# Two-block transformer kernel, one core: gate units, buffers and engines at the start of the seven-product stage

## The chip, the cores and the metric

The kernel runs on 1 core of one Trainium2 chip. The metric is the device time of one execution in microseconds (us). Engine names are those of the profile: PE is TensorE's matmul, PEld its weight load, DVE is VectorE, ACT is ScalarE, POOL is GpSimd, SP is SyncE, which issues nearly all DMAs.

## What is computed

The reference runs two blocks of two layers each on a sequence of 1024 tokens of width 1024, in float32. The change touches only block 1, whose layer is, cut to what matters:

```python
proj = h @ w_in
(aq, ak, av, az, cx, cb, cc, cz, rq, rk, rv, rz, gates) = split(proj)
a = diff_attention(aq, ak, av, ...) * silu(az)
c = short_conv(cx, cb, cc, conv_w) * silu(cz)
r = retention(rq, rk, rv) * silu(rz)
g = sigmoid(gates).reshape(b, s, 3, 1024)
merged = g[:, :, 0] * (a @ w_branch[0])
for i in range(1, 3):
    merged = merged + g[:, :, i] * ((a, c, r)[i] @ w_branch[i])
return x + merged @ w_out
```

The columns `gates` are 3072 wide: 24 units of 128 columns.

## The kernel before

**Arithmetic.** All matmuls are split: an operand x becomes a high part (`c.hi`, a ScalarE copy to the fast matmul type, L144) and a low part x - high (`c.lo`, a subtraction, L151, on VectorE or GpSimd), and a product is three matmuls, high-high, high-low and low-high (`mm3`, L177 to L179). The tokens stand in the free dimension, in two halves f = 0, 1 of 512. The normed input is H[f][k], k = 0 to 7, as tile pairs `hh{f}_{k}`, `hl{f}_{k}`.

**Stages of a block 1 layer.** Attention with the short convolution's units in its gaps (pool C, and A and AZ in it), retention (pool R, also inside C), the gates (pool GS inside pool G), the branch merge (GM inside G), the output product (W). Pools are stacked: pool G opens where pool C began, so its first tiles lie on C's tiles (`cth` 2 KB per partition, then `u`, then `y`, some 4 KB each, all of the convolution), the next ones on R's. With `reuse_waits="tile"` a tile waits only for the older tiles that lie where it lies. Tags of a pool are laid in the order in which they are first asked for. A tag with n buffers hands them out in turn, and a new tile waits for the last reader of the one that held its buffer.

**A plain unit** (`c.unit`, L181) multiplies 128 weight columns with one half: 8 x 3 = 24 matmuls into one of two PSUM banks `pj0`, `pj1` in turn, 48 matmuls for both halves. Weights are loaded to `wr` (2 buffers) and split into `wh` and `wl` (3 buffers each, L166).

**A pair by seven products** (`c.seven`, L230) computes two units with both halves as a 2x2 block product with seven block multiplications in place of eight: 7 x 4 x 3 = 84 matmuls. Its right-hand operands are blocks of H (`B["11"]`, `["21"]`, `["22"]`) and four combinations t1 to t4, computed once per layer; its left-hand ones are made for each pair by `pair_weights` (L198). It opens with product 1 into a `pb` bank, copied to `m` by L242, then product 2 with t2; t3 comes in product 4, t1 in product 5, t4 in product 6. The `pb` tag has four banks.

**The gates stage before** (L810 to L850). Two plain units (44, 45), then 11 pairs. The operands: for each k of 0 to 3, four sums high + low (b12, b22 on VectorE, b11, b21 on GpSimd, L832), four differences (L834, L836, L837, L839) and three splits (t3's low part on GpSimd, those of t2 and t4 on VectorE). They use the tags `m`, `u3`, `c21` and `sc`, two buffers each, and write the tiles t2, t3, t4 (`slot`, pool G). t1 is split later, onto H[1][0 to 3], after the plain units have read those. `gate` (L811) applies tanh on ScalarE to a bank (L813) and stores the result to DRAM (L815); for plain units and for the first gate of a pair it writes to a tile of tag `sc`.

**The merge** (GM, L870 on): for 24 pairs (branch, d) it loads two gates to `gt` (L875), multiplies branch tiles (loaded through `br`, L863) with weights into a `pb` bank, and sums on VectorE (L886 for the first branch). In the kernel before, `gt` is the first tag of GM and lies on the first tags of GS, `m` and `u3`.

**Order.** TensorE runs in program order in these stages (`manual()`); the other engines and SyncE run in the order that a scheduler chose when the program was built, each strictly in that order.

Of the kernel before, what the change touches and what calls it, by code (L numbers as in the profile page):

```python
# [10 lines left out]
F32 = mybir.dt.float32  # L11
# [3 lines left out]
ALU = mybir.AluOpType  # L15
# [4 lines left out]
P = 128  # L20
T = 1024
HW = 512
# [390 lines left out]
def block1_layer(c, a, l, H, rest, last):  # L413
    nc = c.nc
    v, g, s = nc.vector, nc.gpsimd, nc.scalar
# [5 lines left out]
    def load_unit(u):  # L421
        return c.weights(a["w1"][l, u], 1024)

    def manual():
        return c.tc.manual_schedule(engines={mybir.EngineType.PE})
# [103 lines left out]
    with c.scope("C") as pc:  # L529

        with c.scope("A") as pa:
# [14 lines left out]
            gs = c.t(pa, "gs", [P, 1])  # L546
# [259 lines left out]
    with c.scope("G") as pg:  # L806
        def slot(nm, k):
            return tuple(c.t(pg, f"{nm}{x}_{k}", [P, HW], F32R) for x in "hl")

        with c.scope("GS") as pq, manual():  # L810
            def gate(u, f, src, dst=None):  # L811
                dst = c.t(pq, "sc", [P, HW], bufs=2) if dst is None else dst
                s.activation(dst, src, AF.Tanh, scale=0.5)  # L813
                gsp[u, f] = c.dram([P, HW], "sg")
                nc.sync.dma_start(out=gsp[u, f], in_=dst)  # L815

            def split(x, hl, eng):
                c.hi(hl[0], x)
                c.lo(hl[1], x, hl[0], eng=eng)
                return hl  # L820

            def pair(j):
                return c.pair_weights(a["w1"][l, 44 + 2 * j], a["w1"][l, 45 + 2 * j], 1024, pq)

            ws0 = [load_unit(44 + u) for u in range(2)]
            B = {"11": H[0][:4], "21": H[0][4:], "22": H[1][4:], "t1": [], "t2": [], "t3": [], "t4": []}
            t1 = []
            for k in range(4):
                b12, b11, b22, b21 = (c.t(pq, x, [P, HW], F32, 2) for x in ("m", "u3", "c21", "sc"))
                for x, (f, kk), eng in ((b12, (1, k), v), (b22, (1, k + 4), v), (b11, (0, k), g), (b21, (0, k + 4), g)):  # L830
                    hh, hl = H[f][kk]
                    eng.tensor_tensor(out=x, in0=hh.bitcast(F32), in1=hl.bitcast(F32), op=ALU.add)  # L832
                t1.append(c.t(pq, "t1", [P, HW], F32, 4))
                v.tensor_tensor(out=b22, in0=b22, in1=b12, op=ALU.subtract)  # L834
                B["t3"].append(split(b22, slot("t3", k), g))
                v.tensor_tensor(out=t1[k], in0=b12, in1=b11, op=ALU.subtract)  # L836
                v.tensor_tensor(out=b11, in0=b22, in1=b11, op=ALU.add)  # L837
                B["t2"].append(split(b11, slot("t2", k), v))
                v.tensor_tensor(out=b21, in0=b21, in1=b11, op=ALU.subtract)  # L839
                B["t4"].append(split(b21, slot("t4", k), v))  # L840
            for u in range(2):
                for f in range(2):
                    gate(u, f, c.unit(ws0[u], H, f))
                if u == 0:
                    nxt = pair(1)
            for k in range(4):
                B["t1"].append(split(t1[k], c.htile(1, k), v))
            for j in range(1, 12):
                ws, nxt = nxt, pair(j + 1) if j < 11 else None
                c.seven(ws, B, pq, lambda i, f, x: gate(2 * j + i, f, x, None if (i, f) == (0, 0) else x))  # L850


        def branch(br):

            places = ((lambda k: c.htile(0, k), lambda k: slot("t2", k)),
                      (lambda k: c.htile(0, 4 + k), lambda k: slot("t3", k)),
                      (lambda k: slot("t4", k), lambda k: slot("t2", k)))[br]
            out = []
            for f in range(2):
                out.append([])  # L860
                for i in range(4):
                    raw = c.t(pg, "br", [P, HW], bufs=2)
                    nc.sync.dma_start(out=raw, in_=spill[br, i][f])  # L863
                    hl = places[f](i)
                    c.hi(hl[0], raw)
                    c.lo(hl[1], raw, hl[0])
                    out[f].append(hl)
            return out

        with c.scope("GM") as pq, manual():  # L870
            merged, nxt, B = {}, c.weights(a["wb"][l, 0, 0], 512), branch(0)
            for br, d in [(br, d) for br in range(3) for d in range(KD)]:
                gt = [c.t(pq, "gt", [P, HW], bufs=4) for _ in range(2)]
                for f in range(2):
                    nc.sync.dma_start(out=gt[f], in_=gsp[8 * br + d, f])  # L875
                (wh, wl), n = nxt, KD * br + d + 1
                if n < 3 * KD:
                    nxt = c.weights(a["wb"][l, n // KD, n % KD], 512)
                if d == 3 and br < 2:
                    Bn = branch(br + 1)  # L880
                for f in range(2):
                    ps = c.psb()
                    c.product(ps, (wh, wl), 0, B[f])
                    if br == 0:
                        merged[f, d] = c.t(pq, f"mg{f}_{d}", [P, HW])
                        v.scalar_tensor_tensor(out=merged[f, d], in0=gt[f], scalar=1.0, in1=ps, op0=ALU.add, op1=ALU.mult)  # L886
                    else:
                        mt = merged[f, d]
                        v.scalar_tensor_tensor(out=gt[f], in0=gt[f], scalar=1.0, in1=ps, op0=ALU.add, op1=ALU.mult)
                        v.tensor_tensor(out=mt, in0=mt, in1=gt[f], op=ALU.add)  # L890
                if d == KD - 1 and br < 2:
                    B = Bn
            for f in range(2):
                for d in range(KD):
                    mh, ml = c.htile(f, d)
                    c.hi(mh, merged[f, d], 0.5)
                    c.lo(ml, merged[f, d], mh, 0.5)
                    M[f][d] = (mh, ml)
# [807 lines left out]
def tile_kernel(ctx, tc, a, out, stop=99):  # L1706
# [42 lines left out]
    for blk in range(2):  # L1749
        with ExitStack():  # L1750
            for l in range(2):
                if blk == 0:
                    H, rest = block1_layer(c, a, l, H, rest, l == 1)
                else:
                    H, rest = block2_layer(c, a, l, H, rest, out)
                if (blk, l) == (1, 1):
                    rest()
                if stop == 2 * blk + l + 1 and stop < 4:
                    with c.scope("X") as px:
                        for f in range(2):  # L1760
                            for d in range(KD):
                                t = c.t(px, "t", [P, HW], bufs=2)
                                nc.sync.dma_start(out=t, in_=c.xres[f][d])
                                nc.sync.dma_start(out=out[:, d, f * HW:(f + 1) * HW], in_=t)
                    return
# [113 lines left out]
```

## Time and profile before

| | us |
|---|---|
| median of 3 runs (3642.55 to 3646.67) | 3645.57 |
| profiled execution | 3645.27 |
| its span, first to last instruction | 3643.5 |
| TensorE busy | 3454.3 |
| VectorE busy | 2273.3 |
| ScalarE busy | 1449.0 |
| GpSimd busy | 1061.5 |

Matmuls are pipelined: the profile gives one of 128x512 some 0.39 us, while the next starts 0.23 us after it, so the spacing of the starts is what counts. The mean granted clock of TensorE over the span is 0.978 of full speed. The gates stage of layer 1 begins at about 671 us of the span and GM at about 925; those of layer 2 at about 1797 and 2051.

### The profile page before, as it was taken

The page shows a single profiled execution, that of the slowest core. Times are in us where ns is not written, and L with a number is a line of the kernel's source. Part 1 is how long each engine was busy: PE and PEld are TensorE (multiplying, and loading weights), DVE is VectorE, ACT ScalarE, POOL GpSimd, SP SyncE. Part 2 cuts the span into 40 slices and gives each one's busy share as a digit, 9 for nine tenths or more (in the row PEclk, how much of TensorE's full clock was granted, in tenths as well). Part 3 has the DMA queues.
Part 4 walks back from the last instruction along what each step waited for, and adds up shares of the span by engine and source line. Part 5 has one row for each costly group of instructions (what it writes and reads, how often), then busy time and mean ns, then how long its engine had stood idle before and what let it go on. Part 6 is the DMA issues. An engine that isn't in the chain of part 4 may idle for free. (4 is left out here: it accounts for less than half of the span.)

```text
span 3643.5 us, 46305 instructions
## 1 busy us (share of the span) xinstructions
PE 3454.3 (95%) x17348; PEld 2913.6 (80%) x17348; DVE 2273.3 (62%) x4290; ACT 1449.0 (40%) x2575; POOL 1061.5 (29%) x558
## 2 busy tenths in 40 slices
PE   6999999799999899999899999999898999999899
PEld 5888888688788788888778788888777878887787
DVE  7766644732576766645633377588567766965874
ACT  4444333233223444333233324332466534335663
POOL 3222121444234222122434224121322331132223
PEclk9999999899999999999999999999999999999999
DMA  3111211133654111111123545222432342232333
GB/s 112 38 45 46 74 44 50 68 112 102 193 169 143 41 41 47 51 63 53 64 92 111 173 151 162 66 93 76 144 99 79 117 137 70 100 115 92 101 127 108
DMA packets 150370, 343.04 MB, mean 94 GB/s; under 512 B 17457, under 2 KB 30801, under 8 KB 150145
## 3 DMA queue, kind: packets, MB, share of 16 engines
q1 hardware_dynamic: 149312, 338.17, 28.3%
q8 instruction: 137, 2.24, 0.3%
q0 software_dynamic: 544, 1.24, 0.1%
q14 instruction: 89, 0.72, 0.1%
q10 hardware_dynamic: 288, 0.66, 0.1%
HBM read 257.17 MB, written 82.84 MB: 93 GB/s over the span
## 5 line engine op out<-in xcount | busy, mean ns | idle before, releaser
L151 POOL TENSOR_TENSOR wl<-wr,wh 128x1024 fp32r<-128x1024 f32 (+1 forms) x322 | 736.4, 2287 | 2028.7 <-ACT wh L144 2011.5
L177 PE MATMUL pj<-hh,wh 128*128 128x512 f32 x2176 | 881.4, 405 | 61.0 <-ACT sc L813 40.9
L179 PE MATMUL pj<-hh,wl 128*128 128x512 f32 x2176 | 859.2, 395 | 3.8 <-POOL wl L151 3.8
L178 PE MATMUL pj<-hl,wh 128*128 128x512 f32 x2176 | 857.8, 394 | 0.4 <-DVE hl L151 0.4
L144 ACT ACTIVATE wh<-wr 128x1024 fp32r<-128x1024 f32 (+4 forms) x326 | 318.5, 977 | 699.3 <-PE pb L178 292.5
L177 PEld LDWEIGHTS pj<-hh,wh 128*128 128x128 f32 x2176 | 414.7, 191 | 142.8 <-ACT sc L813 41.8
L179 PEld LDWEIGHTS pj<-hh,wl 128*128 128x128 f32 x2176 | 413.5, 190 | 95.9 <-POOL wl L151 5.5
L178 PEld LDWEIGHTS pj<-hl,wh 128*128 128x128 f32 x2176 | 415.0, 191 | 77.6 <-DVE hl L151 0.9
L177 PE MATMUL pb<-hh,wh 128*128 128x512 f32 x904 | 356.6, 394 | 10.4 <-DVE mg L886 7.6
L179 PE MATMUL pb<-hh,wl 128*128 128x512 f32 x904 | 356.1, 394 | 0.9 <-DVE wl L151 0.8
L178 PE MATMUL pb<-hl,wh 128*128 128x512 f32 x904 | 355.4, 393 | 1.6 <-DVE hl L151 1.6
L177 PEld LDWEIGHTS pb<-hh,wh 128*128 128x128 f32 x904 | 171.8, 190 | 47.3 <-ACT wh L144 11.0
L179 PEld LDWEIGHTS pb<-hh,wl 128*128 128x128 f32 x904 | 171.8, 190 | 38.3 <-DVE wl L151 2.6
L178 PEld LDWEIGHTS pb<-hl,wh 128*128 128x128 f32 x904 | 171.9, 190 | 37.4 <-DVE hl L151 1.9
L144 ACT ACTIVATE wth<-pm 128x512 fp32r<-128x512 f32 (+3 forms) x288 | 130.7, 486 | 158.5 <-PE pm L450 94.6
L151 DVE TENSOR_TENSOR wtl<-pm,wth 128x512 fp32r<-128x512 f32 (+3 forms) x288 | 152.4, 550 | 38.6 <-ACT wth L144 36.9
L1153 DVE SCALAR_TENSOR_TENSOR acc<-ya,cwh,acc 128x1024 f32<-128x1024 f32 x120 | 170.6, 1421 | 1.0
L137 DVE CUSTOM_DVE_ANT_0 p<-pb,mk 128x128 f32<-128x128 f32 (+1 forms) x192 | 112.3, 586 | 86.9 <-PE pb L179 43.6
L1567 ACT ACTIVATE p<-p,sm 128x384 f32<-128x384 f32 (+7 forms) x128 | 99.1, 774 | 37.0 <-DVE sm L137 35.5
L1579 PE MATMUL pm<-ident,p 128*128 128x128 f32 x576 | 88.9, 278 | 16.0 <-DVE wtl L151 10.0
L292 DVE TENSOR_TENSOR sqa<-sqa,sq 128x512 f32<-128x512 f32 x56 | 80.7, 1441 | 33.1 <-ACT sq L289 32.7
L151 POOL TENSOR_TENSOR vv<-vt,vv 128x256 fp32r<-128x256 f32 (+1 forms) x32 | 34.4, 1074 | 207.5 <-ACT vv L144 207.5
(475 smaller groups left out, 6809.9 us busy)
## 6 DMA issues: line engine op xcount, KB each, us to landing
wr<-in_w SPq DMA_DIRECT2D x188, 512.0 KB, 3.5
wr<-in_wo SPq DMA_DIRECT2D x64, 512.0 KB, 3.6
gt<-sg SPq DMA_DIRECT2D x96, 256.0 KB, 2.8
br<-sp SPq DMA_DIRECT2D x48, 256.0 KB, 2.9
wr<-in_wb SPq DMA_DIRECT2D x48, 256.0 KB, 2.9
xr<-xn SPq DMA_DIRECT2D x40, 256.0 KB, 2.1
xo<-xr SPq DMA_DIRECT2D x40, 256.0 KB, 2.7
sp<-o SPq DMA_DIRECT2D x32, 256.0 KB, 2.0
```

The costliest lines, as they stand in the source:

```text
L137: self.nc.vector.tensor_tensor_reduce(out=p[:, n0:n1], in0=ps, in1=mask[:, HW + P + n0 - n1:] if n1 == nk else mask[:, 0:HW], scale=1.0, s ...
L144: self.nc.scalar.activation(out, x, AF.Copy)
L151: eng.tensor_tensor(out=out, in0=x, in1=hi.bitcast(F32), op=ALU.subtract)
L177: mm(out, ah, bh, start=first, stop=False, **kw)
L178: mm(out, ah, bl, start=False, stop=False, **kw)
L179: mm(out, al, bh, start=False, stop=last, **kw)
L292: self.nc.vector.tensor_tensor(out=acc, in0=acc, in1=sq, op=ALU.add)
L1153: v.scalar_tensor_tensor(out=acc, in0=ya[:, t_:t_ + T], scalar=cwh[:, 31 * i + t_:31 * i + t_ + 1], in1=acc, op0=ALU.mult, op1=ALU.add)
L1567: s.activation(p[:, :nk], p[:, :nk], AF.Exp, bias=low, scale=-1.0, accum_out=rs[i][:, bl, hh:hh + 1])
L1579: nc.tensor.transpose(ps[:, k, :], p[:, (k0 + k) * P:(k0 + k + 1) * P], c.ident)
```

## The change

The gates stage computes units 44 to 47 plainly and pairs 2 to 11 by seven products (before: units 44 and 45 plainly, pairs 1 to 11). The weights of units 45 to 47 are loaded inside the loop over the units, and the first pair's weights are prepared behind unit 46's gates. Gates get a tag of their own, `gs`, two buffers in pool G; `sc`, moved to pool G, serves only b21. All sums, and t3's low part, move from GpSimd to VectorE. `reserve` fixes the order of the tags: G begins with `gs`, `br` and `sc` (12 KB), so these lie on the convolution's tiles and t2, t3 and t4 on retention's; GS begins with `t1`, `ss`, `wr1`, `s4`; GM begins with `gt`, which thus lies on `t1`.

```diff
+        c.reserve(pg, [("gs", [P, HW], F32, 2), ("br", [P, HW], F32, 2), ("sc", [P, HW], F32, 2)])
         with c.scope("GS") as pq, manual():
+            c.reserve(pq, [("t1", [P, HW], F32, 4), ("ss", [P, 1024], F32, 2), ("wr1", [P, 1024], F32, 2),
+                           ("s4", [P, HW], F32, 2)])
+
             def gate(u, f, src, dst=None):
-                dst = c.t(pq, "sc", [P, HW], bufs=2) if dst is None else dst
+                dst = c.t(pg, "gs", [P, HW], bufs=2) if dst is None else dst
                 s.activation(dst, src, AF.Tanh, scale=0.5)
...
-            ws0 = [load_unit(44 + u) for u in range(2)]
+            ws0 = [load_unit(44)]
...
             for k in range(4):
-                b12, b11, b22, b21 = (c.t(pq, x, [P, HW], F32, 2) for x in ("m", "u3", "c21", "sc"))
-                for x, (f, kk), eng in ((b12, (1, k), v), (b22, (1, k + 4), v), (b11, (0, k), g), (b21, (0, k + 4), g)):
+                b12, b11, b22 = (c.t(pq, x, [P, HW], F32, 2) for x in ("m", "u3", "c21"))
+                b21 = c.t(pg, "sc", [P, HW], bufs=2)
+                for x, (f, kk) in ((b12, (1, k)), (b22, (1, k + 4)), (b11, (0, k)), (b21, (0, k + 4))):
                     hh, hl = H[f][kk]
-                    eng.tensor_tensor(out=x, in0=hh.bitcast(F32), in1=hl.bitcast(F32), op=ALU.add)
+                    v.tensor_tensor(out=x, in0=hh.bitcast(F32), in1=hl.bitcast(F32), op=ALU.add)
                 t1.append(c.t(pq, "t1", [P, HW], F32, 4))
                 v.tensor_tensor(out=b22, in0=b22, in1=b12, op=ALU.subtract)
-                B["t3"].append(split(b22, slot("t3", k), g))
+                B["t3"].append(split(b22, slot("t3", k), v))
...
-            for u in range(2):
+            for u in range(4):
+                ws0.append(load_unit(45 + u) if u < 3 else None)
                 for f in range(2):
                     gate(u, f, c.unit(ws0[u], H, f))
-                if u == 0:
-                    nxt = pair(1)
+                if u == 2:
+                    nxt = pair(2)
             for k in range(4):
                 B["t1"].append(split(t1[k], c.htile(1, k), v))
-            for j in range(1, 12):
+            for j in range(2, 12):
...
         with c.scope("GM") as pq, manual():
+            c.reserve(pq, [("gt", [P, HW], F32, 4)])
```

## Rows read from the trace of the kernel before

**Rows 1.** The page's first part: busy us, share, instructions of each engine.
```profile
PE 3454.3 (95%) x17348; PEld 2913.6 (80%) x17348; DVE 2273.3 (62%) x4290; ACT 1449.0 (40%) x2575; POOL 1061.5 (29%) x558
```

**Rows 2.** Waits of TensorE, whole span: waited for; us in total, times, longest.
```profile
PE pj L177 <- ACT sc L813: 40.9, 2, 20.5
...
PE pb L177 <- DVE mg L886: 7.6, 2, 3.9
...
PE pj L177 <- DVE cth L491: 1.8, 2, 0.9
```

**Rows 3.** Timeline of TensorE, layer 1, plain units: start us, length, line, out<-in, [idle before <-releaser].
```profile
670.79 0.50 PE L177 MATMUL pj<-hh,wh 128*128 128x512 f32 x1 [0.88 <-DVE cth L491]
...
681.58 0.39 PE L179 MATMUL pj<-hh,wl 128*128 128x512 f32 x1
702.45 0.79 PE L177 MATMUL pj<-hh,wh 128*128 128x512 f32 x1 [20.48 <-ACT sc L813]
...
707.24 0.39 PE L179 MATMUL pj<-hh,wl 128*128 128x512 f32 x1
...
715.63 0.39 PE L177 MATMUL pb<-hh,wh 128*128 128x512 f32 x1
```

**Rows 4.** Timeline of ScalarE, layer 1, 680 to 738 us, same columns.
```profile
680.63 0.61 ACT L144 ACTIVATE t3h<-c 128x512 fp32r<-128x512 f32 x1
...
701.79 0.60 ACT L813 ACTIVATE sc<-pj 128x512 f32<-128x512 f32 x1
...
718.55 0.60 ACT L242 ACTIVATE m<-pb 128x512 f32<-128x512 f32 x1 [1.34 <-PE pb L179]
...
737.59 0.60 ACT L242 ACTIVATE m<-pb 128x512 f32<-128x512 f32 x1 [1.36 <-PE pb L179]
```

**Rows 5.** Timeline of VectorE, layer 1, 677 to 702 us.
```profile
677.69 1.77 DVE L492 SCALAR_TENSOR_TENSOR y<-y,cth 128x512 f32<-128x512 f32 x1
...
701.08 0.68 DVE L151 TENSOR_TENSOR t4l<-sc,t4h 128x512 fp32r<-128x512 f32 x1
```

**Rows 6.** Timeline of TensorE, layer 2, the same place.
```profile
1808.10 0.39 PE L179 MATMUL pj<-hh,wl 128*128 128x512 f32 x1
1828.95 0.79 PE L177 MATMUL pj<-hh,wh 128*128 128x512 f32 x1 [20.46 <-ACT sc L813]
...
1833.70 0.40 PE L179 MATMUL pj<-hh,wl 128*128 128x512 f32 x1
```

**Rows 7.** Timeline of TensorE, layer 1, start of the GM stage.
```profile
935.72 0.39 PE L179 MATMUL pb<-t2h,wl 128*128 128x512 f32 x1
940.04 0.77 PE L177 MATMUL pb<-hh,wh 128*128 128x512 f32 x1 [3.93 <-DVE mg L886]
...
946.13 0.39 PE L179 MATMUL pb<-t2h,wl 128*128 128x512 f32 x1
```

**Rows 8.** Timeline of TensorE, layer 2, start of the GM stage.
```profile
2062.22 0.39 PE L179 MATMUL pb<-t2h,wl 128*128 128x512 f32 x1
2066.25 0.77 PE L177 MATMUL pb<-hh,wh 128*128 128x512 f32 x1 [3.65 <-DVE mg L886]
...
2069.24 0.39 PE L178 MATMUL pb<-hl,wh 128*128 128x512 f32 x1
```

**Rows 9.** Timeline of SyncE's DMA issues, layer 1.
```profile
679.86 0.92 SPq L863 DMA_DIRECT2D br<-sp  x2
...
932.49 0.38 SPq L815 DMA_DIRECT2D sg<-m  x1
...
935.61 1.82 SPq L875 DMA_DIRECT2D gt<-sg  x4
```

**Rows 10.** VectorE by line and shape, 640 to 716 us: count, busy us, mean ns.
```profile
L832 DVE TENSOR_TENSOR c<-hh,hl 128x512 f32<-128x512 f32 x4 | 7.0, 1762 | 0.0
...
L839 DVE TENSOR_TENSOR sc<-sc,u 128x512 f32<-128x512 f32 x4 | 2.7, 682 | 0.0
```

**Rows 11.** Timeline of GpSimd, layer 1, 670 us.
```profile
670.90 6.32 POOL L151 TENSOR_TENSOR wl<-wr,wh 128x1024 fp32r<-128x1024 f32 x1 [7.94 <-ACT wh L144]
```

## The prediction

> **What bounds the kernel now.** I read the page's first part first: TensorE is busy for 95% of the span and every other engine for 62% or less [rows 1]. So the time is TensorE's work plus its gaps, and only two things can move it: matmuls added or removed, and gaps opened or closed. The waits of TensorE come next. The largest single cause is L177 waiting for the gate activation L813, 40.9 us in two waits, one in each layer of block 1; L177 behind L886 (the first sums of GM) costs 7.6 us in two waits, and L177 behind the convolution's L491 costs 1.8 us in two [rows 2]. All three lie in or beside the code that is changed. The timelines of the engines around these waits give the rest.
>
> The first wait: the plain units start at 670.79, the first unit's last matmul starts at 681.58, and the second unit's first one only at 702.45 [rows 3]. It needs the first of the two alternating `pj` banks, which gate (0,0) must empty. That gate starts on ScalarE at 701.79 [rows 4], although its product was done 25 us earlier. On VectorE the low part t4l of k=2 starts at 701.08 and runs 0.68 us, to 701.76 [rows 5]. That names the cause in the code. The tag `sc` has two buffers. The four differences b21 take them in turn, so the first gate takes the buffer of k=2 and cannot write until t4l of k=2 has read it. TensorE is thus made to wait for the whole chain of differences, work whose result it doesn't need until later.
>
> Why that chain is late: the first split t3h starts at 680.63 [rows 4]. Tile t3h_0 is the first of pool G, which opens where pool C began, on C's first tile `cth`; the convolution's last L492 reads `cth` from 677.69 to 679.46 [rows 5]. So the operand chain begins only when the convolution ends, though retention's tiles were free long before.
>
> **The pitch.** Two consecutive pairs of the seven-product loop start their L242 at 718.55 and 737.59 [rows 4]: 19.04 us for 7x4x3 = 84 matmuls, 0.2267 us each at full clock.
>
> **Term 1, the gates' own buffers (`gs`) and the operands on retention's memory.** They go together, since either alone would leave the gate behind something late. Layer 1: 702.45 - 681.58 = 20.87 us where one pitch is due, so 20.64 lost. After it the granted clock is low: from 702.45 to 707.24 there are 11 pitches, 4.79 us instead of 2.49, so 2.30 more [rows 3]. Layer 2: 1828.95 - 1808.10 - 0.23 = 20.62, and 11 pitches in 4.75 us, 2.26 more [rows 6]. Together 45.8 us. As a check, 670.79 to 715.63 is 44.84 us for 96 matmuls that need 21.76 [rows 3].
> What is late next: `gs` falls on `cth` and `u`, so gate (0,0) waits for L492, done at 679.46 [rows 5]; with the gate's 0.60 us [rows 4] it is over at about 680.1, and TensorE asks for the bank at 681.8. The spare is 1.7 us. b21 now waits for the last store of y, because `sc` falls on y, but nobody needs t4 before the sixth product of the first pair. I count the gap as gone. If ScalarE's order puts a split that isn't ready ahead of the gate, part of it stays (second rival).
>
> **Term 2, four plain units and one pair fewer.** A pair costs 84 matmuls by seven products and 96 plainly. Per layer 12 more, 12 x 0.2267 = 2.72 us, on the path: 5.4 us slower in all. What goes with it on the other engines (one `pair_weights`: four VectorE operations and four splits; one `seven`: six evacuations) lies beside TensorE and is worth nothing directly. SyncE issues as many loads and gate stores as before; two 512 KB loads now go through `wr` instead of `wr` and `wr1`. Weights for units 46 and 47 can be split when the unit three places earlier in the rotation of `wh` ends, so two units (2 x 48 matmuls, 21.8 us) ahead of use; that covers them. A gate's store is queued on SyncE behind its activation, and a weight load issued behind that store waits with it, for less than one half unit (5.4 us), inside the same cover.
>
> **Term 3, `gt` on `t1`'s memory.** Reserved first in GS, `t1` is what GM's `gt` lies on; before, `gt` lay on `m` and `u3`. `t1` is read for the last time just after the plain units, the other two by the last gate of GS. The first matmul that waits for L886 is the fifth product of GM (four `pb` banks): 940.04 - 935.72 - 0.23 = 4.09 us lost, then 14 pitches in 6.09 us instead of 3.17, 2.92 lost [rows 7]. Layer 2: 3.80, and 7 pitches in 2.99 instead of 1.59, 1.40 lost [rows 8]. Together 12.2 us. The cause is on SyncE: the `gt` loads are issued at 935.61, behind the last store from `m` at 932.49 [rows 9]. After, they are free some 200 us earlier. Will SyncE issue them then? The `br` loads, which belong to the same late stage, were issued at 679.86, as soon as their memory was free [rows 9]; so I say yes, and take the 12.2 us whole (other end: nothing).
>
> **Term 4, differences on VectorE alone.** Eight sums and four low parts per layer leave GpSimd. VectorE then has 4 x 11 = 44 operations for the operands, six of the convolution's tail and four of the first pair's weights: 54. Free, one takes 0.68 us (L839); while GpSimd ran its sums one took 1.76 (L832) [rows 10]. If all of it began only when the plain units do, at 670.79 [rows 3], it would end at 707.5 at 0.68. TensorE's plain units end at 670.79 + 8 x 24 x 0.2267 = 714.3 and t2 is asked for one product later, at 717.0. So it is hidden, with 9.5 us to spare; uncovered, each 0.1 us per operation costs 5.4 us per layer. GpSimd keeps only weights; I take the value near 0.68, since the twelve GpSimd operations that it met are gone.
> The trace shows the two engines slowing each other. [...]
>
> **Sum** against the profiled execution, 3645.27 us (span 3643.5 and 1.8 around it): - 45.8 + 5.4 - 12.2 = - 52.6, so 3592.7; the median of the runs is 0.3 above the profiled one: 3593. The convolution's L491 wait (1.8 us) I leave as it is, with up to 2 us per layer either way for the reordered VectorE queue: own range 3588 to 3598. Chance 0.60.
>
> **Rivals.**
> 1. *The GM gap stays.* `gt` can be free and still be issued late, behind `br` loads in SyncE's one queue, or L886 can sit in VectorE's queue behind a split that waits for `br`. For it: the `gt` loads stood behind such a load already. Against: the `br` precedent. Price 12.2: 3605. Chance 0.13.
> 2. *Part of the first gap stays.* The spare of 1.7 us before gate (0,0) is small, and L491 and L492 sit in the same VectorE queue as the sums. A shift of 1 to 10 us beyond the spare, per layer, with up to 2.3 us of low clock: 3595 to 3618. Chance 0.14. This is also the case in which the change doesn't wholly do what it says.
> 3. *GpSimd is kept out.* One weight's low part already took 6.32 us beside a full VectorE [rows 11]. If none ran before VectorE is through, at 707.5 by Term 4's late start, unit 46's (wanted at 692.6) would be 17 us late; started as early as the memory allows, it is hidden. Between these: with half of its work done earlier, VectorE is through at about 690, unit 46's low part would end 6.32 us later, and TensorE would wait some 4 us per layer: 3601. Chance 0.05.
> 4. *Slower.* VectorE is contended throughout. At 1.76 us per operation, 54 end at 765.8, 48.8 us after t2 is wanted; per layer + 48.8 + 2.3 + 2.7 - 22.9 - 6.1 = + 24.8, so 3695. It decides at a lateness of 24 us, that is (717.0 + 24.0 - 670.79)/54 = 1.30 us per operation. For it: those 1.76 us. Against: some five GpSimd operations are left in that stretch, and even at 6.32 us each they block 32 us, 1.26 per operation. Chance 0.05.
> 5. *Better*: the L491 wait goes too, and VectorE's freer queue closes others: 3588 or less. Chance 0.03.
>
> **Range.** 3587 to 3609 leaves out the fourth case, half of the second and part of the fifth. A measurement of this kernel can tell about 0.2%, 7.3 us, from no change. The forecast, rivals one to three and five are faster by more: 0.95, of which I move 0.02 to within 0.2%, for a second rival much longer than priced; 0.05 is slower.
>
> **What would show it.** Term 1: no wait of L177 for L813, and the plain units from first matmul to the first of `seven` in 43.5 us. Term 2: 24 more matmuls, ten pairs per layer at 19.04 us. Term 3: `gt` loads issued before GS ends and no wait for L886. Term 4: no wait of `seven` for t2 to t4, and L832 near 0.7 us. A gate on ScalarE that starts after 681.2 in layer 1, or a t2l that ends after 717 would make the prediction wrong.

## The result, and the profile after

The changed kernel takes 3604.48 us, median of 4 runs (3600.25 to 3612.88), beside 3645.37 us for the kernel before on the same chip: a ratio of 0.9892, 95% interval 0.987 to 0.9913. That is 41 us faster, 11 us short of the forecast of 3593 and inside the range. The profiled execution is the longest of the four, 3612.88 us (span 3610.6, granted clock 0.982 on average); a second set of runs gave 3606.52.

In the changed code the lines have moved: the gate's activation is L817, its store L819, the sums L837, the differences L839 to L844, the `br` loads L869, the `gt` loads L882, the first sums of GM L893.

First part of the page of the changed kernel (busy us, share, instructions):

```profile
PE 3459.2 (96%) x17372; PEld 2919.1 (81%) x17372; DVE 2248.3 (62%) x4296; ACT 1444.6 (40%) x2569; POOL 1023.4 (28%) x530
```

Beside [rows 1]: 24 matmuls more, 12 per layer as Term 2 says, and 28 instructions fewer on GpSimd.

Waits of TensorE in the changed kernel (waited for; us in total, times, longest); they answer to [rows 2]:

```profile
PE pb L177 <- DVE mg L893: 8.9, 2, 5.1
...
PE pj L177 <- ACT gs L817: 5.4, 2, 2.8
```

The gate's wait has shrunk from 40.9 us to 5.4, GM's has not shrunk at all, and the convolution's wait for L491 is not in the list any more.

TensorE in the changed kernel, both layers: the first matmul of the plain units, the gap inside them, the first and the last matmul with t2, the gap in GM, the last matmul with t4. They answer to [rows 3], [rows 6], [rows 7] and [rows 8]; columns as there:

```profile
671.59 0.39 PE L177 MATMUL pj<-hh,wh 128*128 128x512 f32 x1
...
707.15 0.50 PE L177 MATMUL pj<-hh,wh 128*128 128x512 f32 x1 [2.77 <-ACT gs L817]
...
722.49 0.39 PE L177 MATMUL pj<-t2h,wh 128*128 128x512 f32 x1
...
895.89 0.39 PE L177 MATMUL pj<-t2h,wh 128*128 128x512 f32 x1
...
924.99 0.76 PE L177 MATMUL pb<-hh,wh 128*128 128x512 f32 x1 [3.77 <-DVE mg L893]
...
1043.97 0.39 PE L177 MATMUL pb<-t4h,wh 128*128 128x512 f32 x1
...
1780.65 0.39 PE L177 MATMUL pj<-hh,wh 128*128 128x512 f32 x1
...
1816.13 0.50 PE L177 MATMUL pj<-hh,wh 128*128 128x512 f32 x1 [2.68 <-ACT gs L817]
...
1829.87 0.39 PE L177 MATMUL pj<-t2h,wh 128*128 128x512 f32 x1
...
2003.27 0.39 PE L177 MATMUL pj<-t2h,wh 128*128 128x512 f32 x1
...
2033.67 0.77 PE L177 MATMUL pb<-hh,wh 128*128 128x512 f32 x1 [5.09 <-DVE mg L893]
...
2152.94 0.39 PE L177 MATMUL pb<-t4h,wh 128*128 128x512 f32 x1
```

Differences of these starts divide the execution into stretches; the same points read in the other traces give this table (us). "All the rest" is what remains between TensorE's first matmul and the start of its last one. "Forecast" is the prediction's own terms put to the stretches; "again" is the second set of runs of the changed kernel; the last two columns belong to experiments 9 and 8 below.

| stretch | before | forecast | after | again | late `gt` | late `gt`, low parts on VectorE |
|---|---|---|---|---|---|---|
| plain units to first t2, layer 1 | 47.56 | 46.25 | 50.90 | 49.31 | 50.06 | 46.24 |
| the same, layer 2 | 47.55 | 46.25 | 49.22 | 49.22 | 50.03 | 46.24 |
| first to last t2, each layer | 192.44 | 173.40 | 173.40 | 173.40 | 173.40 | 178.0 |
| last t2 to last t4 (GM's start is in it), layer 1 | 148.49 | 141.48 | 148.08 | 147.21 | 141.75 | 141.67 |
| the same, layer 2 | 146.68 | 141.48 | 149.67 | 147.48 | 142.89 | 141.76 |
| all the rest | 2851.9 | 2851.9 | 2849.1 | 2845.2 | 2844.1 | 2844.9 |

Take the second set's trace: against the forecast the plain units lack 3.06 and 2.97 us, GM lacks 5.73 and 6.00, and the rest is 6.7 better, so 11.1 us in all: all but 0.3 us of the distance between the forecast's 3592.7 and that execution's 3604.1. So there are two misses and one windfall to explain.

**The gap that is left in the plain units.** It stands ahead of unit 47's first product, which needs the bank that unit 46's first gate empties, and not at gate (0,0). ScalarE in the changed kernel, layer 1: the first gate, the last t4 split, and the gate that TensorE waited for:

```profile
677.23 0.60 ACT L817 ACTIVATE gs<-pj 128x512 f32<-128x512 f32 x1 [1.99 <-PE pj L179]
...
705.99 0.63 ACT L144 ACTIVATE t4h<-sc 128x512 fp32r<-128x512 f32 x1 [1.18 <-DVE sc L844]
706.52 0.58 ACT L817 ACTIVATE gs<-pj 128x512 f32<-128x512 f32 x1
```

Gate (0,0) follows its product at once. The late gate stands behind a split in ScalarE's order, and that split waits for a difference on VectorE. VectorE in the same stretch:

```profile
692.54 0.70 DVE L842 TENSOR_TENSOR u<-c,u 128x512 f32<-128x512 f32 x1
699.95 0.69 DVE L208 TENSOR_TENSOR ss<-wr,wr 128x512 f32<-128x512 f32 x1 [6.72 <-DMA wr<-in_w]
...
705.27 0.68 DVE L844 TENSOR_TENSOR sc<-sc,u 128x512 f32<-128x512 f32 x1
```

VectorE stood still for 6.72 us because the first operation of a weight pair (L208) was at the head of its queue and its load had not come; the last differences were queued behind it. SyncE: the `br` loads, that weight load, the last gate store from `m`, and the first `gt` loads:

```profile
676.57 1.77 SPq L869 DMA_DIRECT2D br<-sp  x2
...
695.52 0.33 SPq L203 DMA_DIRECT2D wr<-in_w  x1
...
917.55 0.38 SPq L819 DMA_DIRECT2D sg<-m  x1
...
920.47 1.85 SPq L882 DMA_DIRECT2D gt<-sg  x4
```

The load is issued at 695.52, when a `wr` buffer comes free. GpSimd, which reads `wr` last:

```profile
672.75 2.40 POOL L151 TENSOR_TENSOR wl<-wr,wh 128x1024 fp32r<-128x1024 f32 x1 [8.48 <-ACT wh L144]
683.63 14.22 POOL L151 TENSOR_TENSOR wl<-wr,wh 128x1024 fp32r<-128x1024 f32 x2 [8.48 <-ACT wh L144]
```

One low part takes 2.40 us (so too at 720.94, where VectorE stands still); two from 683.63 on take 14.22 together, through the time in which VectorE runs back to back (until 693.2 by the row above). Nearly all of the excess belongs to the first, unit 47's: it gives back the buffer that is loaded at 695.52, for pair 3, some 12 us after it began, while the second ends 2.3 us later than that. That is the chain: GpSimd kept out, `wr` late, load late, VectorE blocked by its own queue, split late, gate late, 2.77 us of TensorE.

**The gap in GM.** VectorE in the changed kernel at GM's start, layer 1:

```profile
923.55 0.69 DVE L151 TENSOR_TENSOR t3l<-br,t3h 128x512 fp32r<-128x512 f32 x1 [1.76 <-ACT t3h L144]
924.16 0.68 DVE L893 SCALAR_TENSOR_TENSOR mg<-gt,pb 128x512 f32<-128x512 f32 x1
925.34 2.00 DVE L893 SCALAR_TENSOR_TENSOR mg<-gt,pb 128x512 f32<-128x512 f32 x3 [0.50 <-DMA gt<-sg]
```

The `gt` loads go out at 920.47, behind the last gate store, in the same place as before [rows 9], though what they overwrite was read for the last time soon after the plain units (by 718.6). They are not what ended last, though: the first sum follows the low part of the third t3 tile without idle time, and that one had waited for its split and so for a `br` load; only the second sum waited for `gt`, 0.50 us. VectorE in the kernel before, at the same place:

```profile
938.61 0.69 DVE L151 TENSOR_TENSOR t3l<-br,t3h 128x512 fp32r<-128x512 f32 x1 [1.72 <-ACT t3h L144]
939.22 1.28 DVE L886 SCALAR_TENSOR_TENSOR mg<-gt,pb 128x512 f32<-128x512 f32 x2
```

So there too the sum stood behind a split in VectorE's order, beside loads that were issued late; the prediction's "The cause is on SyncE" named one of the two.

### The profile page after: what moved, and what is told of

The parts are those of the page before. It is cut to its first block, busy times and chain, and to the rows that moved or that the text cites. A ratio compares the mean times of both kernels' runs of the same rounds, so it can differ in the third digit from the quotient of the medians.

```text
span 3610.6 us, 46289 instructions
## 1 busy us (share of the span) xinstructions
PE 3459.2 (96%) x17372; PEld 2919.1 (81%) x17372; DVE 2248.3 (62%) x4296; ACT 1444.6 (40%) x2569; POOL 1023.4 (28%) x530
## 3 DMA queue, kind: packets, MB, share of 16 engines
q0 software_dynamic: 544, 1.24, 0.1%
## 5 line engine op out<-in xcount | busy, mean ns | idle before, releaser
L151 POOL TENSOR_TENSOR wl<-wr,wh 128x1024 fp32r<-128x1024 f32 (+1 forms) x322 | 747.9, 2323 | 2014.2 <-ACT wh L144 1997.2
L177 PE MATMUL pj<-hh,wh 128*128 128x512 f32 x2240 | 905.1, 404 | 23.8 <-DVE zm L1386 13.8
L179 PE MATMUL pj<-hh,wl 128*128 128x512 f32 x2240 | 883.5, 394 | 3.8 <-POOL wl L151 3.8
L178 PE MATMUL pj<-hl,wh 128*128 128x512 f32 x2240 | 882.2, 394 | 0.4 <-DVE hl L151 0.4
L177 PEld LDWEIGHTS pj<-hh,wh 128*128 128x128 f32 x2240 | 426.4, 190 | 107.0 <-DVE zm L1386 15.1
L179 PEld LDWEIGHTS pj<-hh,wl 128*128 128x128 f32 x2240 | 425.2, 190 | 98.3 <-POOL wl L151 5.5
L178 PEld LDWEIGHTS pj<-hl,wh 128*128 128x128 f32 x2240 | 426.6, 190 | 79.8 <-DVE hl L151 0.9
L177 PE MATMUL pb<-hh,wh 128*128 128x512 f32 x880 | 347.3, 395 | 11.5 <-DVE mg L893 8.9
L179 PE MATMUL pb<-hh,wl 128*128 128x512 f32 x880 | 347.4, 395 | 0.9 <-DVE wl L151 0.8
L178 PE MATMUL pb<-hl,wh 128*128 128x512 f32 x880 | 346.5, 394 | 1.6 <-DVE hl L151 1.6
```

Of the source, the lines that this page charges most:

```text
L151: eng.tensor_tensor(out=out, in0=x, in1=hi.bitcast(F32), op=ALU.subtract)
L177: mm(out, ah, bh, start=first, stop=False, **kw)
L178: mm(out, ah, bl, start=False, stop=False, **kw)
L179: mm(out, al, bh, start=False, stop=last, **kw)
```

## The experiments

Each kernel ran beside the kernel before on the same chip; ratios are to that, with their 95% intervals.

**0. The changed kernel once more.** No edit.

> The changed kernel itself, as the measure for the other three on the same chip. Four earlier executions took 3600.3, 3600.8, 3608.2 and 3612.9 us with mean granted clocks of 0.986, 0.985, 0.983 and 0.982. Theory: the spread is low-clock stretches behind short gaps of TensorE that some executions have and others don't. Then time and mean granted clock go together here too, with a median near 3604 and executions between 3599 and 3613. Rival: the spread is in the waits themselves (a DMA landing sooner or later); then the clock doesn't order the times.

3606.52 us (3603.22 to 3609.68), 0.9898 (0.9883 to 0.9913). Waits of 2.76 and 2.68 us for `gs`, 3.92 and 4.16 for L893. Over all eight executions the time follows the mean granted clock, from 3600.25 us at 0.986 to 3612.88 at 0.982. The median near 3605 is therefore no accident of one trace.

**1. `gt` in the outer pool.** t1 and `gt` become one tag of pool G, which is open all the time; `gt` still lies on t1's memory, and the tiles behind it in pool G move on by its size.

```diff
-        c.reserve(pg, [("gs", ...), ("br", ...), ("sc", ...)])
+        c.reserve(pg, [("gs", ...), ("br", ...), ("sc", ...), ("gt", [P, HW], F32, 4)])
...
-                t1.append(c.t(pq, "t1", [P, HW], F32, 4))
+                t1.append(c.t(pg, "gt", [P, HW], F32, 4))
...
-                gt = [c.t(pq, "gt", [P, HW], bufs=4) for _ in range(2)]
+                gt = [c.t(pg, "gt", [P, HW], bufs=4) for _ in range(2)]
```

> One edit: t1 and gt share one tag of pool G, which is open all the time, instead of gt lying on t1's memory in a pool of its own that opens after GS. Theory A: the GM gap (4.16 + 5.47 us between starts in the profiled execution, and 3 us of low clock after each) is there because the gt loads, free of any wait, are issued on SyncE only behind the last gate's store and the br loads; with the tag in the open pool they are issued some 200 us earlier, the L893 wait goes, and the kernel is 10 to 15 us faster than the changed one, about 3591. Rival B: the loads are early, but the first L893 stands in VectorE's queue behind the splits of br tiles, which wait for their own loads; then the gap stays within 2 us of what it was and the time is that of the changed kernel.

3594.54 us (3590.15 to 3597.3), 0.9864 (0.9849 to 0.9879), 12 us below run 0. SyncE in this kernel:

```profile
713.61 4.32 SPq L881 DMA_DIRECT2D gt<-sg  x4
719.80 0.32 SPq L819 DMA_DIRECT2D sg<-gs  x1
721.80 0.33 SPq L203 DMA_DIRECT2D wr<-in_w  x1
```

VectorE at GM's start in the same kernel:

```profile
918.08 0.69 DVE L151 TENSOR_TENSOR t3l<-br,t3h 128x512 fp32r<-128x512 f32 x1 [2.62 <-ACT t3h L144]
918.69 1.28 DVE L892 SCALAR_TENSOR_TENSOR mg<-gt,pb 128x512 f32<-128x512 f32 x2
```

The first `gt` loads are issued 207 us earlier, and the sums now stand behind the first t3 split, where the changed kernel put them behind the third. TensorE's wait for them is gone in layer 1 and 1.00 us in layer 2. The waits for `gs` are 1.78 and 1.71 us here, and in layer 2 the first pair waits 1.95 us for L237, as in run 3 below. So memory that is free early was not what GM's gap lacked: the place in the orders made it. The edit moved two of them together, the loads on SyncE and the sums on VectorE; which of the two is worth more was not separated.

**2. Low parts of units 46 and 47 on VectorE.**

```diff
-        return c.weights(a["w1"][l, u], 1024)
+        return c.weights(a["w1"][l, u], 1024, v if u in (46, 47) else None)
```

> One edit: the low parts of the weights of units 46 and 47 are made on VectorE (0.7 to 1.3 us each) instead of GpSimd. Theory A: the wait of L177 for gate (2,0), 2.8 us in each layer, is the end of a chain that begins with GpSimd's low part of unit 47's weights taking some 12 us beside a full VectorE: the wr buffer comes free late, the next load is issued at 695.5, L208 waits for it 6.7 us at the head of VectorE's queue, and the t4 splits that stand before gate (2,0) on ScalarE come late. Then L208's wait and L177's wait for L817 go (below 0.5 us per layer), and the kernel is 5 to 9 us faster than the changed one, about 3597. Rival B: the gate is late only because ScalarE's order has it behind the t4 splits, and these are late by the length of VectorE's work; then the wait stays at 2 to 3 us, or grows by the 2 us that are added to VectorE.

3603.46 us (3600.18 to 3605.6), 0.989 (0.9873 to 0.9906). No wait for `gs` is left, VectorE doesn't wait for the load, and the plain units take 46.24 us in both layers, the forecast's figure. That confirms the chain. But the median is only 3 us below run 0 with overlapping intervals; 5 to 9 were expected. Against run 0's trace the plain units win 6.0 us, and all the rest, which the edit doesn't touch, loses 4.5. GpSimd in this kernel:

```profile
688.33 14.19 POOL L151 TENSOR_TENSOR w4l<-s,w4h 128x512 fp32r<-128x512 f32 x1 [24.80 <-ACT w4h L144]
...
704.84 1.27 POOL L151 TENSOR_TENSOR w4l<-s,w4h 128x512 fp32r<-128x512 f32 x1
```

The same operation takes 1.27 us when VectorE pauses and 14.19 beside it: the late low part has moved to a place where nobody waits for it.

**3. Both edits.**

> The two edits together. If both theories A hold, neither of the two gaps is left in either layer, the gains add, 15 to 22 us against the changed kernel, about 3586, and the spread between executions shrinks to that of the kernel before (some 4 us), because there is less idle time for the clock to fall in. If one of the two rivals holds, it is as fast as the better of the two alone.

3600.58 us (3598.4 to 3605.13), 0.9884 (0.9869 to 0.9898): 6 us more than the first edit alone, which neither case of the expectation had. Waits of TensorE in this kernel:

```profile
PE pb L177 <- DVE u L237: 6.8, 2, 3.4
```

VectorE ahead of that wait, and GpSimd beside it, layer 1:

```profile
723.66 2.27 DVE L208 TENSOR_TENSOR ss<-wr,wr 128x512 f32<-128x512 f32 x1 [3.60 <-DMA wr<-in_w]
726.04 2.68 DVE L209 TENSOR_TENSOR wr<-wr 128x512 f32<-128x512 f32 x1
...
730.09 0.68 DVE L237 TENSOR_TENSOR u<-pb,m 128x512 f32<-128x512 f32 x1
...
722.98 2.40 POOL L151 TENSOR_TENSOR wl<-wr,wh 128x1024 fp32r<-128x1024 f32 x1 [4.11 <-ACT wh L144]
725.71 2.45 POOL L151 TENSOR_TENSOR wl<-ss,wh 128x1024 fp32r<-128x1024 f32 x1 [0.33 <-ACT wh L144]
```

A bank of the first pair is emptied by L237 at 730.09, behind a later pair's L208, which waits for its load again; here four `gt` loads stood ahead of that load on SyncE. L208 and L209 then take 2.27 and 2.68 us where 0.69 is usual: each ends some 0.55 us behind the GpSimd operation that it met (2.40 and 2.45 us), so here it is VectorE that is held up. The gains don't add because the same kind of wait, a weight pair at the head of VectorE's queue, opens one pair later: against run 1's trace the plain units win 5.8 us and the pairs lose 6.7. In these stretches the two traces are thus alike within 1 us; where the 6 us between the medians lie is not shown.

**4. Own gate buffers alone**, in the kernel before:

```diff
-                dst = c.t(pq, "sc", [P, HW], bufs=2) if dst is None else dst
+                dst = c.t(pq, "gs", [P, HW], bufs=2) if dst is None else dst
```

> The kernel before with one part of the change: gates write to a tag gs of their own, everything else as before (two plain units, pairs 1 to 11, sums on GpSimd too, operands on the convolution's memory). The prediction counted this part and the operands' place as one term, because either alone would leave something late. Theory A (so): the wait for L813 goes, but t2's last low part, ready at 702.5 in the kernel before, is wanted at about 695.3 when the plain units run through, so a wait of some 7 to 9 us stands at the second product of the first pair; per layer 20.6 us become 7 to 9, and the time is 3617 to 3624. Rival B: the own buffers are worth the whole term; the wait goes and nothing takes its place, 3645 - 46 = about 3599. Rival C: ScalarE's order holds the gate back behind the splits anyway; 3640 or more.

3628.03 us (3627.23 to 3630.7), 0.9953 (0.9938 to 0.9967): 18 us gained, a little less than the 3617 to 3624 expected. The plain units shrink by 18 us per layer (from 47.56 to 28.94 and from 47.55 to 29.53), the pairs grow by 11. TensorE's waits in this kernel:

```profile
PE pj L177 <- ACT gs L813: 8.9, 2, 4.7
...
PE pb L177 <- DVE u L237: 6.8, 2, 3.4
...
PE pb L177 <- ACT m L242: 3.0, 2, 1.5
```

The wait moves from the second unit to the first pair, as "either alone would leave the gate behind something late" supposed; part of it, the 6.8 us for L237, is the weight pair at the head of VectorE's queue again.

**5. Two plain units, pairs 1 to 11**, with the rest of the change kept.

```diff
-            for u in range(4):
-                ws0.append(load_unit(45 + u) if u < 3 else None)
+            for u in range(2):
+                ws0.append(load_unit(45 + u) if u < 1 else None)
...
-                if u == 2:
-                    nxt = pair(2)
+                if u == 0:
+                    nxt = pair(1)
```

> The changed kernel with its fourth part undone: two plain units and pairs 1 to 11 again, all else as changed. It saves 12 matmuls per layer, 2.7 us, and takes away 21.8 us of cover. Theory A: the cover is needed. In the changed kernel t2's last low part ends at 706.5 in layer 1, with 6.7 us of that from a load wait; without two of the units t2 is wanted at some 696, so TensorE waits 5 to 11 us per layer at the second product, with low clock behind it: 5 to 20 us slower than the changed kernel, 3610 to 3625. Rival B: VectorE orders the operands earlier and nothing waits; then it is 5.4 us faster than the changed one, about 3600.

3611.23 us (3609.2 to 3612.32), 0.9905 (0.989 to 0.9919). Theory A had the place and the size of the wait, but not what is waited for; TensorE in this kernel, layer 1:

```profile
702.63 0.79 PE L179 MATMUL pj<-t2h,wl 128*128 128x512 f32 x1 [6.79 <-POOL wl L151]
```

The first pair has its t2 in time; what it lacks is its own low weights: one low part on GpSimd takes 17.97 us there, from 684.61 on, beside a VectorE without pauses. By the ratios this kernel is 3 to 5 us above the changed one (0.9892 and 0.9898), and the intervals overlap: the two more plain units bring back the 5.4 us that they cost and hardly more.

**6. The sums b11 and b21 and t3's low parts back on GpSimd.**

> The changed kernel with its last part undone: b11, b21 and t3's low part on GpSimd again. Theory A: VectorE alone is what brings the operands in time; with GpSimd the operations of both run at 1.7 us each, t2's last low part comes after 717 and TensorE waits for it, 5 us or more slower than the changed kernel, above 3610. Rival B: with four plain units there is cover enough for either, and the chain of the load wait (GpSimd's low part of 12 us beside a full VectorE) may even be gone since VectorE has pauses; then it is within 4 us of the changed kernel, and the wait for L817 is smaller than 2.7 us.

3619.67 us (3612.76 to 3622.71), 0.9931 (0.9915 to 0.9948), 12 to 14 us above the changed kernel by the ratios. Waits of TensorE in it:

```profile
PE pj L177 <- ACT gs L817: 12.3, 4, 5.9
```

The size is what was expected; the wait sits at the gates, which stand behind the late splits, not at t2.

**7 and 9. `gt` in the outer pool, its first four loads issued behind pair 8**, late enough to stay clear of the first pairs, early enough for GM. Low parts stay on GpSimd in both runs, whatever the first one's name says.

```diff
+                if j == 8:
+                    with c.behind(mybir.EngineType.SP):
+                        for d in range(2):
+                            early.append([c.t(pg, "gt", [P, HW], bufs=4) for _ in range(2)])
+                            for f in range(2):
+                                nc.sync.dma_start(out=early[d][f], in_=gsp[d, f])
```

> The changed kernel with t1 and gt on one tag of the open pool G, as in e1, but the first four gt loads issued on SyncE behind the loads of pair 8, far from the first pair. (The low parts stay on GpSimd, as in the changed kernel.) e3 was 6 us slower than e1 and showed a wait of 3.4 us at the first pair's t4 product, behind L208 on VectorE, whose weight load stood on SyncE behind the four gt loads. Theory A: those loads at that place are its cause; e1 has them there too, in layer 2 (1.95 us at the same product). Then here no wait at the t4 product and none for L893 are left, the wait for L817 stays at 2.7 us per layer, and the time is 3591 to 3595, e1's or up to 3 us less. Rival B: the order of VectorE's queue is the cause, whatever SyncE does; then a wait of 2 to 3 us at the t4 product stays in one layer at least.

> The changed kernel with `gt` in the outer pool and its first four loads issued behind pair 8, low parts of the weights on GpSimd as in the changed kernel: the same kernel as the run before, for comparison on the same chip. Both theories: 3590 to 3596 us, waits of L177 for `gs` of 1.7 to 1.9 us per layer.

3592.67 us (3590.28 to 3595.82), 0.9855 (0.984 to 0.987), and on another chip 3592.96 (3591.92 to 3594.73), 0.9854 (0.9837 to 0.987). The waits for `gs` are 1.83 and 1.81 us in the second of these, GM's 1.17 in layer 2 alone, and no pair waits for L237, as theory A had it. This version is below both kernels, and at the forecast's time, but not by the forecast's terms: by the table its plain units lack 3.8 us in each layer, and all the rest is 7.8 us better.

**8. The same with the low parts of units 46 and 47 on VectorE.**

> The changed kernel with both repairs: `gt` in the outer pool, its first four loads issued behind pair 8, and the low parts of the weights of units 46 and 47 on VectorE. Theory A (waits add up once the `gt` loads don't stand ahead of the weight load that the first pair needs): no wait of L177 for `gs`, none of `seven` for t4, none for L893; the version with the late `gt` alone still had 1.80 and 1.76 us for `gs`, so this one is up to 3.6 us below it, some 3588 to 3592 us. Rival B: the two more operations on VectorE push the first pair's own splits, as they did with the early `gt` loads; then a wait of 2 to 4 us per layer for t4 is there, and the time is 3592 to 3600.

3598.76 us (3595.32 to 3601.2), 0.987 (0.9855 to 0.9885): the rival was right. TensorE in this kernel, the first pair of each layer:

```profile
731.13 0.50 PE L177 MATMUL pb<-t4h,wh 128*128 128x512 f32 x1 [2.69 <-DVE u L237]
...
1833.60 0.50 PE L177 MATMUL pb<-t4h,wh 128*128 128x512 f32 x1 [2.67 <-DVE u L237]
```

VectorE ahead of it, layer 1:

```profile
724.26 2.70 DVE L209 TENSOR_TENSOR wr<-wr 128x512 f32<-128x512 f32 x1
727.00 2.75 DVE L210 TENSOR_TENSOR ss<-wr,wr 128x512 f32<-128x512 f32 x1
```

There is no `gt` load near it this time; four gate stores stand ahead of that weight load on SyncE instead, so run 3's account by the `gt` loads was only half of it. The load wait of L208 is 2.38 us; L209 and L210, each beside a low part of 2.4 us on GpSimd, add 4.1 us to it. In run 2, where the pair's four operations take 0.69 us each in layer 1, no such wait stands. By the table the plain units win 3.8 us per layer and the pairs lose 4.6. These profiled executions differ by 0.6 us, this one the fastest of its four and run 9's the slowest; why the medians differ by 6 is not settled by them.

**10. Gates back on `sc`**, the rest of the change kept.

```diff
-                dst = c.t(pg, "gs", [P, HW], bufs=2) if dst is None else dst
+                dst = c.t(pg, "sc", [P, HW], bufs=2) if dst is None else dst
```

> The changed kernel with its gates back on the tag `sc`, which they share with b21; `gs` is reserved but not used, so the operand tiles lie where the change puts them. Theory A (own gate buffers are what removed the first gap; operands that start earlier alone do not): gate (0,0) can write only when t4l of k=2 has read its buffer, at some 700 to 708 us, so TensorE stands 18 to 27 us per layer before the second plain unit and runs at the low clock behind it: 3640 to 3660 us. Rival B (operands that start earlier are most of it): the gate waits less than 10 us per layer, 3610 to 3625 us.

3655.69 us (3649.28 to 3658.29), 1.0025 (1.0013 to 1.0037): the whole gain is gone, and a little more. Waits of TensorE:

```profile
PE pj L177 <- ACT sc L817: 49.4, 2, 24.7
```

ScalarE in this kernel, the gate that TensorE waited for, behind the low part t4l of k=2:

```profile
704.40 1.26 ACT L817 ACTIVATE sc<-pj 128x512 f32<-128x512 f32 x2 [1.18 <-DVE t4l L151]
```

Together with run 4: the buffers alone give 18 us, the rest of the change, early operands among it, gives nothing without them, and all together close all but 3 us of the gap per layer in run 0's trace.

## Why the prediction came out as it did

The time lies in the range, above the forecast's own 3588 to 3598. That it meets the first rival's 3605 so closely is luck: Term 1 lost 6 us, and all the rest gained 6.7.

**Term 1 was right in its mechanism, and 6 us too good.** The gaps of [rows 3] and [rows 6] are gone: four plain units take 50.90 and 49.22 us where two took 47.56 and 47.55. The cause named from [rows 5], the shared buffer and t4l of k=2, is shown by run 10; that the buffers alone leave something late, by run 4. What the operands' place is worth by itself is not shown: run 4 lacks the two units and the move to VectorE as well, and no run undoes the place alone. The check before gate (0,0) was too careful: L492 now ends at 675.7 and not at 679.46, and the gate starts at 677.23. What was missed stands 30 us later. The text looked for what is late next at the first gate only; there are eight, all in one queue on ScalarE with the splits.

**Term 2 was right.** 24 more matmuls, and 173.40 us from the first to the last t2 where 192.44 less one pitch of 19.04 are 173.40. Its cover was claimed as 21.8 us for the weights of units 46 and 47. That held for those units, but the wait came through the `wr` buffer that unit 47 hands on to pair 3, which the term named only as "two 512 KB loads now go through `wr`" and costed at nothing. Run 5 shows that the two units about pay for themselves, by covering late low parts on GpSimd.

**Term 3 failed: 12.2 us taken, none given; the first rival came true.** The step that fell is "The `br` loads, which belong to the same late stage, were issued at 679.86, as soon as their memory was free [rows 9]; so I say yes". The `gt` loads were issued at 920.47, some 200 us behind the last reader of their memory. `br` is a tag of pool G, open since the stage began; `gt` was a tag of GM, which is opened when GS is closed. Run 1 puts `gt` into G: loads at 713.61 in place of 920.47, and 12 us. Free memory lets a load go early; the order made for the queue decides if it does. Both forms of the rival are in the trace, the late loads and the sum behind a split that waits for `br`, and the second was there before as well, which the term didn't read.

**Term 4 was right for what it counted.** The sums that took 1.76 us on average in [rows 10] take 0.69 (the means of the operand lines lie between 0.68 and 1.12), t2's last low part ends at 706.55 (705.87 and 0.68) against 717.0 wanted, and run 6 shows VectorE alone is worth 12 to 14 us. Its by-effect was the third rival. "One weight's low part already took 6.32 us beside a full VectorE" was sized well short: some 12 us in the changed kernel, 17.97 in run 5, and 14.19 in run 2 for one of half that size. Nor were those 6.32 us the time of a low part by itself, which is 2.40 in the changed kernel: it began at 670.90 and ended at 677.22, beside a VectorE without pauses, 2.35 us after the start of VectorE's L491 (674.87). Why it ended there is not shown. Its price was put at 4 us per layer and is 3.0 in run 0 by the table, but as a chain through five queues, not as a late weight.

**The windfall.** L491's wait [rows 2], left as it is in the sum, is gone; with the time around it that is some 1 us per layer. That leaves 4 to 5 us of the 6.7 in "all the rest", in code that the change doesn't touch; the same row is 2.2 us better in run 2 and 7.8 in run 9, so it moves from run to run. Over all thirteen traces it lies between 2841.1 and 2851.9 us, with the kernel before at the top, and its last part, behind the last t4 of layer 2, between 1446.6 and 1458.3. Its cause stays open, and the 6.7 us are luck as far as is known.

**The slower rival** needed 1.30 us per operation on VectorE; the means of the operand lines end at 1.12, L492's is 1.24, and most are 0.69. That each GpSimd operation left would block VectorE for 6.32 us was an estimate; beside a low part of 2.96 us in the kernel before a VectorE operation of 0.68 took 2.88, and beside some 2.4 in runs 3 and 8 it took 2.27 to 2.75.

## What to carry to other kernels

- When memory is freed earlier so that a load can start earlier, look up where the load stands in its queue's order, and where its first reader stands in its own. Here the loads for a tile of a pool that wasn't open yet went out only when that pool came, though their memory had been free for 200 us.
- A queue that mixes work for now with preparation for later (splits and gates on ScalarE, differences and weight pairs on VectorE) stops at the first operand that is late, here VectorE for 6.72 us. Follow each late input through every queue behind it, and put one edit in at a time: two repairs that each removed a wait were together 6 us slower than the first one alone.
- Moving work from GpSimd to VectorE can make GpSimd's remaining work late. Here what was left there ended, in runs 2 and 5, 1.16 and 2.20 us into VectorE's next pause, with 1.27 and 2.40 us of its own; and in runs 3 and 8 VectorE's operations were the longer ones, up to 2.75 us in place of 0.69.

## What the runs showed of the hardware

A GpSimd operation beside a VectorE without pauses took no fixed multiple of its own time; in runs 2 and 5 it ended about its own duration after VectorE's row of operations. In run 2, 1.27 us became 14.19: through 21 VectorE operations, the last of which ended at 701.36, and 1.16 us more. In run 5, 2.40 became 17.97, from 684.61 to 702.58: through 26, the last of which ended at 700.38, and 2.20 us more. In the changed kernel two of 2.40 took 14.22, the first of them some 12. VectorE's own operations kept to 0.69 us meanwhile. It can be VectorE that takes longer: in runs 3 and 8 operations of 0.69 us took 2.27 to 2.75 beside GpSimd operations of 2.4. And it can be both: in the kernel before, from 682.57 to 690.99 in layer 1, VectorE's operations took 1.74 or 1.75 us each and those of GpSimd beside them 1.70 or 1.71; the 1.76 of [rows 10] is a mean over four that took 0.68, 2.88, 1.75 and 1.75. What decides between these cases the traces don't show.

Behind some of TensorE's short idle times the granted clock was 0.50, behind others 1.00. Windows of the changed kernel behind the gaps of the plain units (layers 1 and 2) and of GM; the column ahead of the last two is the granted clock as a share of full speed:

```profile
709.10:711.60 2.50, 2.50 (x7) 1.93 (x6) 0.00 (x0) 1.96 (x3) 1.90 (x2) 0.50 0.00 0
925.60:930.20 4.60, 4.60 (x12) 3.57 (x11) 2.65 (x5) 1.26 (x2) 0.00 (x0) 0.50 1.02 378
1816.20:1821.00 4.80, 4.80 (x21) 3.98 (x22) 1.74 (x3) 2.07 (x3) 2.31 (x2) 1.00 0.17 63
```

Behind 2.77 us idle in layer 1 it is 0.50; behind 2.68 us idle at the same place in layer 2 it stays 1.00. Nor does the length of the gap decide it in these traces: behind 2.76 us at the same place in run 0 the clock stays at 1.00, behind 1.83 us in run 9 it is 0.50 (712.6 to 715.6). Gaps of 3.77 and 5.09 us in GM were both followed by 0.50, the second by some thirteen matmuls spaced 0.43 us, where 0.23 is the spacing at 1.00. By the table the plain units lose 3.0 us where the clock stays, and 4.7 in layer 1 of the changed kernel, which can be one reason why its executions spread over 12.6 us.
